# Moving the copy of the last transposed tile behind a weights' cast, and turning two tiles in one go

## The chip, the cores and the metric

The kernel runs on one core of one Trainium2 chip. A core has TensorE (PE: matrix products and transposes through the array), VectorE (DVE), ScalarE (ACT), GpSimd (POOL), SyncE (SP, which here only issues transfers) and 16 DMA engines that move data between the chip's memory and the core's SBUF. The metric is the device time of one launch in microseconds (us), the median of several runs. Each engine takes its instructions strictly in the order in which they stand in the program, so an instruction that waits also holds up what stands behind it.

## The reference

One layer of a hybrid decoder for 512 tokens and a model width of 2048, in float32:

```
h  = rmsnorm(x)
y  = concat[StickBreakingAttn(6 heads), ShortGatedConv(4 groups), GatedDeltaNet(6 heads)](h @ w_in)
x  = x + y @ w_out                                # output projection
x  = x + square(relu(rmsnorm(x) @ w_up)) @ w_down # MLP, width 8192
out = rmsnorm(x)
```

The products keep float32 precision by splitting each operand into a rounded "hi" part (a cast on ACT) and the remainder "lo" (a subtraction on DVE); a product is then three matmuls: hi by hi, hi by lo, lo by hi.

## The kernel before

The program runs through five stages: the input projections with the three mixers (to about 740 us), the output projection (745 to 895 us), the MLP's up products (895 to 1535 us), its down products (to 2147 us) and the final norm. The order of each engine's instructions is fixed when the program is built, by a scheduler that simulates the engines; `behind(...)` tells it that what is issued inside must stand after the given instructions, and `tc.high_priority(...)` lets the preparation of weights move ahead of other work.

**Output projection** (the loop over `m` at L785). For each of 16 blocks of 128 output columns, `gemm` (L129) runs four chunks; a chunk is a load of weights into `raw` (SP), their split into `whi` (ACT, L103) and `wlo` (DVE, L104) and 12 matmuls (L116 to L118). The result is added to x on DVE (L793), giving the tile `x1[m]`. Since the last stage needs x with tokens on partitions, `turn(m)` (L767) transposes the tile by four 128x128 transposes into PSUM (L774) and copies it on ACT into `turned` (L775); after each second tile SP writes `turned` to the scratch tensor `xs` (L777). Before, both tiles of a pair are asked for ahead of the product of block `m`.

**Start of the up products** (`up_pair`, g = 0). The up and down products use a fast scheme with seven products instead of eight, taken in the order 1, 2, 5, 6, 3, 4, 7. Each product is 24 matmuls over eight k-tiles. Products 1 and 2 use weights that were loaded like those of the output projection. The weights of product 5, `W_8784`, are the cast (ACT, L841) and the remainder (DVE, L842) of `q_8786`, a tile that is loaded by SP (L849) and then added to by an accumulating transfer that POOL issues (L865). Product 6 uses `W_8936`, split from the same `q_8786` after DVE has added `q_8782` to it (L859). Between products 2 and 5 PE transposes the last tile, `turn(KT - 1, pbank(2))` (L958). After product 5, `scale_rows` sums squares over partitions by a matmul with ones (L836). Product 4 needs the second half of the normed activations, which goes through memory: `rows` splits it (tile `t22`) and SP writes it to `x22` (L783), and `x4_prep` loads it back in four steps (L900), as `whi` and `wlo`; the last step, `whi_8901` and `wlo_8902`, holds the k-tiles 6 and 7. Its matmuls stand on PE among those of the first product of the next group.

SP carries all these loads and stores in one queue, in a fixed order. A transfer also waits until an earlier one of the same semaphore (one of eight, in turn) has landed.

Of the kernel before, what the change touches and what calls it, by code (L numbers as in the profile page):

```python
# [2 lines left out]

# [13 lines left out]
P = 128  # L17
T = 512
NB = T // P
D = 2048  # L20
KT = D // P
# [6 lines left out]
CHUNK_KT = 4  # L28
# [26 lines left out]
def trunk(ctx, tc, xT, wv1, wv2, wa, wo, wu, wd, vec, wf, out, dbg=None):  # L55
    nc = tc.nc
    V, S, G, PE = nc.vector, nc.scalar, nc.gpsimd, nc.tensor
# [15 lines left out]
    def mmps():  # L73
        pool, bufs = pool_of_mm
        return pool.tile([P, 512], F32, name="mm", tag="mm", bufs=bufs)

    def xps(tag):
        pool, bufs = pool_of[tag]
        return pool.tile([P, 512], F32, name=tag, tag=tag, bufs=bufs)
# [8 lines left out]
    def tmp(n=512):  # L88
        return per.tile([P, n], F32, name="tmp", tag="tmp", bufs=4)

    def big():
        return big_pool.tile([P, 2, 512], F32R, name="big", tag="big", bufs=16, align_bytes=256)
# [4 lines left out]
    def wload(src, n, prio=None):  # L97
        with tc.high_priority(WPRIO if prio is None else prio):
            raw = per.tile([P, 512], F32, name="raw", tag="raw", bufs=4)
            nc.sync.dma_start(out=raw[:, :n], in_=src)  # L100
            hi = per.tile([P, 512], F32R, name="whi", tag="whi", bufs=4, align_bytes=256)
            lo = per.tile([P, 512], F32R, name="wlo", tag="wlo", bufs=4, align_bytes=256)
            S.copy(out=hi[:, :n], in_=raw[:, :n])  # L103
            V.tensor_tensor(out=lo[:, :n], in0=raw[:, :n], in1=hi[:, :n].bitcast(F32), op=ALU.subtract)  # L104
        return hi, lo

    def behind(*ins):

        ctx = ExitStack()
        for i in ins:  # L110
            ctx.enter_context(tc.issue_after(i.ins))
        return ctx

    def mm3(p, lh, ll, rh, rl, first, last, more=False):

        PE.matmul(p, lhsT=lh, rhs=rh, start=first, stop=False, skip_group_check=more)  # L116
        PE.matmul(p, lhsT=lh, rhs=rl, start=False, stop=False, skip_group_check=more)  # L117
        return PE.matmul(p, lhsT=ll, rhs=rh, start=False, stop=last, skip_group_check=more)  # L118

    def gemm_chunk(p, src, acts, c, prio=None):  # L120

        ks = slice(c * CHUNK_KT, (c + 1) * CHUNK_KT)
        hi, lo = wload(src[:, ks, :].rearrange("p k f -> p (k f)"), CHUNK_KT * P, prio)
        for k in range(CHUNK_KT):
            s = slice(k * P, (k + 1) * P)
            a = acts[c * CHUNK_KT + k]
            mm3(p, hi[:, s], lo[:, s], a[:, 0], a[:, 1], c + k == 0, c * CHUNK_KT + k == KT - 1)

    def gemm(src, acts):  # L129
        p = mmps()  # L130
        for c in range(KT // CHUNK_KT):
            gemm_chunk(p, src, acts, c)
        return p

    def silu(x, s):
# [27 lines left out]
    def col(c):  # L163
        return vc[:, c:c + 1]
# [29 lines left out]
    for k in range(KT):  # L194
        hi, lo = wload(wv1[:, k, :], 268, 0)
        xr = big_pool.tile([P, 512], F32, name="xr", tag="xr", bufs=6)
        nc.sync.dma_start(out=xr, in_=xT[:, k, :])
        a = big()
# [4 lines left out]
        for b in range(NB):  # L203
            s = slice(b * P, (b + 1) * P)
# [15 lines left out]
    p = xps("r")  # L220
# [3 lines left out]
    p = xps("r")  # L224
# [90 lines left out]
    p = xps("r")  # L315
# [414 lines left out]
    yh = []  # L730
    for k in ORDER:
        a = big()
# [7 lines left out]
    def half_split(o, src):  # L740
        S.copy(out=o[:, :, 0], in_=src)
        V.tensor_tensor(out=o[:, :, 1], in0=src, in1=o[:, :, 0].bitcast(F32), op=ALU.subtract)
# [8 lines left out]
    def sums(o, A11, A12, A21, A22):  # L751

        sub(o[:, 0], A22, A21)
        nsub(o[:, 1], o[:, 0], A11)
        nsub(o[:, 2], o[:, 1], A12)
        sub(o[:, 3], A11, A21)
# [7 lines left out]
    Rb = per.tile([P, 512], F32, name="Rb")  # L764
    turned = {}

    def turn(m, p=None):  # L767

        if m % 2 == 0:
            turned["o"] = late.tile([P, NB, 2 * P], F32, name="turned", tag="turned", bufs=1)  # L770
        o = turned["o"]
        p = xps("t") if p is None else p
        for b in range(NB):
            PE.transpose(p[:, b * P:(b + 1) * P], x1[m][:, b * P:(b + 1) * P], ident)  # L774
        S.copy(out=o[:, :, m % 2 * P:m % 2 * P + P], in_=p.rearrange("p (b f) -> p b f", b=NB))  # L775
        if m % 2:
            nc.sync.dma_start(out=xs[:, :, (m - 1) * P:(m + 1) * P], in_=o)  # L777

# [6 lines left out]
    for m in range(KT):  # L785
        xr = big_pool.tile([P, 512], F32, name="xr", tag="xr", bufs=6)
        nc.sync.dma_start(out=xr, in_=xT[:, m, :])
        if m == KT - 1 or m and m % 2 == 0:
            for q in range(m - m % 2 - 2 + 2 * (m % 2), m):
                turn(q)  # L790
        p = gemm(wo[m], yh)
        x = big_pool.tile([P, 512], F32, name="x1", tag="xr", bufs=6) if m < KT - 1 else tmp()
        V.tensor_tensor(out=x, in0=p, in1=xr, op=ALU.add)  # L793
        y = tmp()
        S.activation(out=y, in_=x, func=AF.Copy, scale=col(C_N2 + m))
        if m == 0:
            S.activation(out=Rb, in_=x, func=AF.Square)
        else:
            sq = tmp()
            S.activation(out=sq, in_=x, func=AF.Square)  # L800
            if m < KT - 1:
                G.tensor_tensor(out=Rb, in0=Rb, in1=sq, op=ALU.add)
        x1.append(x)
        yw.append(y)
        i = m // 2
        half_split(XP[i][:, m % 2:m % 2 + 1], y[:, :HT].unsqueeze(1))
        if m % 2:
            t = xsum = late.tile([P, 4, HT], F32, name="xsum", tag="xsum", bufs=2)
            y0 = yw[m - 1]
            sums(t, y0[:, :HT], y[:, :HT], y0[:, HT:], y[:, HT:])  # L810
            if m < KT - 1:
                rows(i, t, y)
# [16 lines left out]
    def pbank(n):  # L829
        return psu.tile([P, 512], F32, name="pu", tag={1: "uX", 2: "uY", 4: "uY", 5: "uZ"}[n], bufs=2)  # L830
# [79 lines left out]
    def up_pair(g):  # L910

        st = {}
        z = [per.tile([P, 512], F32, name="raw", tag="raw", bufs=4) for _ in range(2)]
        keep, banks, Ws = {}, {}, {}

        def mms(n, lo, hi):
            p = banks[n]
            for i in range(lo, hi):
                xh, xl = x_side(n, i)
                s = slice(i * P, (i + 1) * P)  # L920
                if isinstance(Ws[n], list):
                    s = slice(i % 4 * P, i % 4 * P + P)
                    w = [a[:, s] for a in Ws[n][i // 4]]
                else:
                    w = [Ws[n][:, 0, s], Ws[n][:, 1, s]]
                last = mm3(p, *w, xh, xl, n in (1, 2, 4, 5) and i == 0, i == KP - 1,
                           n in (6, 7, 3))
            return last

        def take(n):  # L930
            p = banks[n]
            if n in (1, 5, 6, 4):
                keep[n] = tmp()[:, :HT]
                S.copy(out=keep[n], in_=p)
                return
            for o, k in {2: ((z[0][:, :HT], 1),), 3: ((z[1][:, :HT], 6),),
                         7: ((z[0][:, HT:], 4), (z[1][:, HT:], 5))}[n]:
                V.tensor_tensor(out=o, in0=p, in1=keep[k], op=ALU.add)

        src = lambda kh, d: wu[g, kh, d]  # L940
        for n in UP:
            if n not in Ws:
                Ws[n] = w_prep(n, st, src, False, g > 0 or n not in (1, 2))
            if g == 0 and n in (1, 2):
                Ws[n] = [wload(wu[0, n - 1, 0][:, 512 * c:512 * c + 512], 512) for c in range(2)]
            banks[n] = pbank(n)[:, :HT] if n in (1, 2, 4, 5) else banks[{6: 1, 7: 1, 3: 5}[n]]
            if g == 0 and n == 1:
                mms(1, 0, KP - 1)
                continue
            if g == 0 and n == 2:  # L950
                Ws[5] = w_prep(5, st, src, False)
                with behind(*st["split"]):
                    rows(KP - 1, xsum, yw[-1])
                mms(2, 0, KP - 1)
                mms(1, KP - 1, KP)
                take(1)
                with behind(mms(2, KP - 1, KP)):
                    turn(KT - 1, pbank(2))  # L958
                take(2)
                continue  # L960
            else:
                if g == 0 and n == 5:
                    x4_prep()
                last = mms(n, 0, KP)
                if g == 0 and n == 5:
                    scale_rows(last)
            take(n)
        h = ahead.pop("h", None) or h_tile()

        def finish():  # L970
            to_h(g, h, z)

        if g < FF // P // 2 - 1:
            finish()
        else:
            rest.append(finish)
# [273 lines left out]
```

## Time and profile before

| | |
|---|---|
| median of 3 runs | 2159.11 us (2157.95 to 2159.48) |
| the profiled execution, its own time | 2158.76 us |
| its span, from first to last instruction | 2157.1 us |
| PE busy | 2137.5 us, 99% of the span |
| DVE busy | 1661.0 us, 77% |
| ACT busy | 1071.5 us, 50% |
| DMA, share of the hardware queue and of POOL's queue | 41.1% and 13.5% |
| mean granted clock of TensorE | 0.998 |

Columns of a timeline row: start in us, duration in us, engine, line, operation, tile written <- tiles read, shape, count, and in brackets the idle time before it with what ended it. In a table of stretches an engine's number is its busy time in us; PEclk is the clock granted to TensorE (1.00 is 2.4 GHz, 0.50 is 1.2 GHz), the DMA share is that of the 16 engines. Durations overlap where an engine pipelines.

### The profile page before, as it was taken

To read this page: it belongs to the slowest core of one execution; us is meant where nothing else is said; L and a number is where in the kernel's file an instruction comes from. 1 tells how busy PE (TensorE), PEld (TensorE's weight loads), DVE (VectorE), ACT (ScalarE), POOL (GpSimd) and SP (SyncE) were. 2 spreads that over 40 slices of the span, in tenths; PEclk is the share of its full clock that TensorE was granted. 3 is DMA by queue.
4 is the path that set the end of the run, shared out by engine and by line. 5 is a ranking of instruction groups with operands and counts; after the bars stand their busy time and mean duration, and the time that the engine had idled before them with its cause. 6 is when DMAs were issued, how large, how long until landed. Compare 5 with 4: busy or idle time off the path is not lost.

```text
span 2157.1 us, 33102 instructions
## 1 busy us (share of the span) xinstructions
PE 2137.5 (99%) x12674; PEld 1883.5 (87%) x12674; DVE 1661.0 (77%) x2360; ACT 1071.5 (50%) x1629; POOL 132.5 (6%) x188
## 2 busy tenths in 40 slices
PE   9999999999999999999999999999999999999998
PEld 8887888888989888899999999999888888888886
DVE  6677978644656765588788788878998898898897
ACT  5646766333434544444444545444544454444455
POOL 0000000000000011100000000000001000000101
PEclk9999999999999999999999999999999999999999
DMA  5333233222222255766666666666997777787674
GB/s 185 108 99 97 82 92 92 87 93 85 86 79 88 93 162 161 246 189 186 196 188 171 198 196 176 177 199 190 287 306 185 240 223 200 201 228 224 184 214 117
DMA packets 160718, 356.42 MB, mean 165 GB/s; under 512 B 20272, under 2 KB 62256, under 8 KB 160432
## 3 DMA queue, kind: packets, MB, share of 16 engines
q1 hardware_dynamic: 146304, 302.93, 41.1%
q0 software_dynamic: 13968, 50.86, 13.5%
q8 instruction: 99, 1.62, 0.3%
q14 instruction: 59, 0.48, 0.1%
q10 hardware_dynamic: 288, 0.52, 0.1%
HBM read 308.90 MB, written 45.36 MB: 164 GB/s over the span
## 4 chain that ended last, share of the span: by engine, by line
PE 95%; DVE 2%; ACT 1%; DMA 1%; issue 1%; SPq 0%; DVEq 0%; ACTq 0%
PE mm L117 11%; PE mm L116 11%; PE mm L118 11%; PE pu L118 10%; PE pu L116 10%; PE pu L117 10%; PE pp L117 9%; PE pp L118 9%; PE pp L116 9%; PE mm L280 1%; PE mm L281 1%; PE mm L279 1%; PE i L404 1%; DVE W L842 0%; DMA q<-in_wd_dram 0%
## 5 line engine op out<-in xcount | busy, mean ns | idle before, releaser
L841 ACT CAST W<-q 128x1024 fp32r<-128x1024 f32 x446 | 465.0, 1050 | 571.5 <-PE pp L118 261.8
L842 DVE TENSOR_TENSOR W<-q,W 128x1024 fp32r<-128x1024 f32 x446 | 540.7, 1221 | 125.3 <-ACT W L841 121.1
L116 PE MATMUL mm<-big,whi 128*128 128x512 f32 x1024 | 404.6, 395 | 1.8 <-ACT whi L103 1.2
L117 PE MATMUL mm<-big,whi 128*128 128x512 f32 x1024 | 403.9, 394 | 0.0
L118 PE MATMUL mm<-big,wlo 128*128 128x512 f32 x1024 | 402.4, 393 | 0.0
L117 PE MATMUL pp<-W,A 128*128 128x512 f32 x888 | 345.8, 389 | 0.4 <-DVE W L842 0.4
L118 PE MATMUL pp<-W,A 128*128 128x512 f32 x888 | 345.6, 389 | 0.4 <-DVE A L842 0.4
L116 PE MATMUL pp<-W,A 128*128 128x512 f32 x888 | 343.1, 389 | 0.8 <-ACT W L841 0.8
L104 DVE TENSOR_TENSOR wlo<-raw,whi 128x512 fp32r<-128x512 f32 (+1 forms) x292 | 196.8, 675 | 159.4 <-ACT whi L103 151.9
L103 ACT CAST whi<-raw 128x512 fp32r<-128x512 f32 (+1 forms) x292 | 176.8, 607 | 277.0 <-PE mm L117 237.6
L116 PE MATMUL pu<-XS,W 128*128 128x256 f32 x1024 | 287.8, 281 | 1.8 <-ACT W L841 1.6
L118 PE MATMUL pu<-XS,W 128*128 128x256 f32 x1024 | 287.1, 281 | 0.8 <-DVE W L842 0.8
L117 PE MATMUL pu<-XS,W 128*128 128x256 f32 x1024 | 287.2, 280 | 0.0
L116 PEld LDWEIGHTS mm<-big,whi 128*128 128x128 f32 x1024 | 192.4, 188 | 41.4 <-ACT whi L103 1.8
L117 PEld LDWEIGHTS mm<-big,whi 128*128 128x128 f32 x1024 | 192.5, 188 | 39.1 <-DVE big L734 0.3
L118 PEld LDWEIGHTS mm<-big,wlo 128*128 128x128 f32 x1024 | 192.4, 188 | 38.9
L116 PEld LDWEIGHTS pp<-W,A 128*128 128x128 f32 x888 | 166.7, 188 | 36.0 <-ACT W L841 1.5
L117 PEld LDWEIGHTS pp<-W,A 128*128 128x128 f32 x888 | 166.7, 188 | 35.8 <-DVE W L842 1.0
L118 PEld LDWEIGHTS pp<-W,A 128*128 128x128 f32 x888 | 166.7, 188 | 35.2 <-DVE A L842 0.8
L116 PEld LDWEIGHTS pu<-XS,W 128*128 128x128 f32 x1024 | 193.2, 189 | 2.8 <-ACT W L841 2.3
L859 DVE TENSOR_TENSOR q<-q 128x1024 f32<-128x1024 f32 x159 | 193.7, 1219 | 1.3
L118 PEld LDWEIGHTS pu<-XS,W 128*128 128x128 f32 x1024 | 193.1, 189 | 1.0 <-DVE W L842 1.0
(302 smaller groups left out, 3283.5 us busy)
## 6 DMA issues: line engine op xcount, KB each, us to landing
q<-in_wu_dram SPq DMA_DIRECT2D x128, 512.0 KB, 4.5
q<-in_wd_dram SPq DMA_DIRECT2D x128, 512.0 KB, 5.6
raw<-in_wa_dram SPq DMA_DIRECT2D x192, 256.0 KB, 2.9
hs<-h SPq DMA_DIRECT2D x32, 1024.0 KB, 5.5
q<-in_wd_dram POOLq DMA_DIRECT2D x64, 512.0 KB, 7.1
ha<-hs SPq DMA_DIRECT2D x55, 512.0 KB, 6.5
q<-in_wu_dram POOLq DMA_DIRECT2D x33, 512.0 KB, 5.5
raw<-in_wo_dram SPq DMA_DIRECT2D x64, 256.0 KB, 2.9
```

Of the source, the lines that this page charges most:

```text
L103: S.copy(out=hi[:, :n], in_=raw[:, :n])
L104: V.tensor_tensor(out=lo[:, :n], in0=raw[:, :n], in1=hi[:, :n].bitcast(F32), op=ALU.subtract)
L116: PE.matmul(p, lhsT=lh, rhs=rh, start=first, stop=False, skip_group_check=more)
L117: PE.matmul(p, lhsT=lh, rhs=rl, start=False, stop=False, skip_group_check=more)
L118: return PE.matmul(p, lhsT=ll, rhs=rh, start=False, stop=last, skip_group_check=more)
L279: PE.matmul(o, lhsT=xw[k][:, 0, s], rhs=hi[:, ws], start=k == 0 and b % 2 == 0, stop=False)
L280: PE.matmul(o, lhsT=xw[k][:, 0, s], rhs=lo[:, ws], start=False, stop=False)
L281: PE.matmul(o, lhsT=xw[k][:, 1, s], rhs=hi[:, ws], start=False, stop=k == KT - 1 and b % 2 == 1)
L404: PE.matmul(pv[:, b], lhsT=kq[:, 2 * c + b, 0], rhs=kq[:, 2 * c + b], start=True, stop=True)
L841: return (S.copy(out=o[:, 0], in_=src), V.tensor_tensor(out=o[:, 1], in0=src, in1=o[:, 0].bitcast(F32), op=ALU.subtract))
L842: V.tensor_tensor(out=o[:, 1], in0=src, in1=o[:, 0].bitcast(F32), op=ALU.subtract))
L859: on_v = lambda t, u: V.tensor_tensor(out=t, in0=t, in1=u, op=ALU.add)
```

## The change

Two places change. The copy of the last transposed tile is issued behind the split of product 5's weights (`after=st["split"]`), where it stood ahead of it on ACT. And the transposes of a pair of tiles in the output projection are issued together after the second chunk of the following product (`between`), where one tile's stood at the product's start and the other's after its second chunk.

```diff
-            mm3(p, hi[:, s], lo[:, s], a[:, 0], a[:, 1], c + k == 0, c * CHUNK_KT + k == KT - 1)
+            last = mm3(p, hi[:, s], lo[:, s], a[:, 0], a[:, 1], c + k == 0, c * CHUNK_KT + k == KT - 1)
+        return last
...
-    def gemm(src, acts):
+    def gemm(src, acts, between=()):
         p = mmps()
         for c in range(KT // CHUNK_KT):
-            gemm_chunk(p, src, acts, c)
+            last = gemm_chunk(p, src, acts, c)
+            if c == 1 and between:
+                with behind(last):
+                    for f in between:
+                        f()
         return p
...
-    def turn(m, p=None):
+    def turn(m, p=None, after=()):
...
-        S.copy(out=o[:, :, m % 2 * P:m % 2 * P + P], in_=p.rearrange("p (b f) -> p b f", b=NB))
+        with behind(*after):
+            S.copy(out=o[:, :, m % 2 * P:m % 2 * P + P], in_=p.rearrange("p (b f) -> p b f", b=NB))
...
-        if m == KT - 1 or m and m % 2 == 0:
-            for q in range(m - m % 2 - 2 + 2 * (m % 2), m):
-                turn(q)
-        p = gemm(wo[m], yh)
+        turns = range(m - m % 2 - 2 + 2 * (m % 2), m) if m == KT - 1 or m and m % 2 == 0 else ()
+        p = gemm(wo[m], yh, [partial(turn, q) for q in turns])
...
                 with behind(mms(2, KP - 1, KP)):
-                    turn(KT - 1, pbank(2))
+                    turn(KT - 1, pbank(2), st["split"])
```

ACT's order between products 2 and 5, before (`turned_8666` is the copy of the last tile, `W_8784` the cast for product 5, `XS_7227` and `t22_8847` the split of the last activations, `tmp_8875` the copy of product 1's result):

```order
L741 CAST XP_7219<-tmp_8748 128x256
L775 COPY turned_8666<-pu_8880 128x4x128
L841 CAST W_8784<-q_8786 128x1024
L741 CAST XS_7227<-xsum_8754 128x4x256
L741 CAST t22_8847<-tmp_8748 128x256
L934 COPY tmp_8875<-pu_8808 128x256
L841 CAST W_8936<-q_8786 128x1024
```

The same place now (lines of the changed kernel are 6 to 8 higher):

```order
L748 CAST XP_7219<-tmp_8748 128x256
L847 CAST W_8784<-q_8786 128x1024
L748 CAST XS_7227<-xsum_8754 128x4x256
L748 CAST t22_8847<-tmp_8748 128x256
L940 COPY tmp_8875<-pu_8808 128x256
L783 COPY turned_8703<-pu_8880 128x4x128
L847 CAST W_8936<-q_8786 128x1024
```

The copy has moved back by four instructions, and nothing else on ACT has moved here. DVE's order is the same in the whole program.

SP's queue at that time, before (`q_` are weights of the next groups, `xs` is written from the last pair of turned tiles, `x22` from the last `t22`, and `whi_8901` is the first half of product 4's last load):

```order
L849 DMA q_9070<-in_wu_dram 128x1024
L777 DMA xs_7228<-turned_8666 512x1x256
L849 DMA q_9293<-in_wu_dram 128x1024
L783 DMA x22_7229<-t22_8847 128x512
L849 DMA q_9299<-in_wu_dram 128x1024
L849 DMA q_9295<-in_wu_dram 128x1024
L849 DMA q_9522<-in_wu_dram 128x1024
L900 DMA whi_8901<-x22_7229 128x2x256
```

And now:

```order
L855 DMA q_9070<-in_wu_dram 128x1024
L855 DMA q_9293<-in_wu_dram 128x1024
L785 DMA xs_7228<-turned_8703 512x1x256
L791 DMA x22_7229<-t22_8847 128x512
L855 DMA q_9299<-in_wu_dram 128x1024
L855 DMA q_9295<-in_wu_dram 128x1024
L855 DMA q_9522<-in_wu_dram 128x1024
L906 DMA whi_8901<-x22_7229 128x2x256
```

The store to `xs` and one weights' load have changed places; `x22` and `whi_8901` stand where they stood.

PE in the output projection, now, at the first pair whose place has changed (before, the first four transposes stood 24 matmuls earlier, at the product's start):

```order
L118 MATMUL mm_7603<-big_7181,whi_7624 128x512
L119 MATMUL mm_7603<-big_7181,wlo_7625 128x512
L781 MATMUL t_7641<-ident_78,x1_7497 128x128 x4
L781 MATMUL t_7647<-ident_78,x1_7581 128x128 x4
L117 MATMUL mm_7603<-big_7184,whi_7656 128x512
```

Six pairs now stand like this; the number of instructions is the same on every engine.

## Rows read from the trace of the kernel before

**Rows 1.** The page, busy time and share of the span by engine.

```profile
PE 2137.5 (99%) x12674; PEld 1883.5 (87%) x12674; DVE 1661.0 (77%) x2360; ACT 1071.5 (50%) x1629; POOL 132.5 (6%) x188
```

**Rows 2.** All waits of PE from 740 to 915 us: total, times, longest.

```profile
PE pu L116 <- ACT W L841: 1.6, 1, 1.6
PE pu L118 <- DVE W L842: 0.8, 1, 0.8
```

**Rows 3.** Timeline of ACT around the copy of the last tile.

```profile
896.75 0.39 ACT L741 CAST XP<-tmp 128x256 fp32r<-128x256 f32 x1
901.01 0.59 ACT L775 COPY turned<-pu 128x512 f32<-128x512 f32 x1 [3.87 <-PE pu L774]
901.50 1.05 ACT L841 CAST W<-q 128x1024 fp32r<-128x1024 f32 x1
902.44 1.05 ACT L741 CAST XS<-xsum 128x1024 fp32r<-128x1024 f32 x1
...
906.44 1.99 ACT L841 CAST W<-q 128x1024 fp32r<-128x1024 f32 x2 [2.37 <-DVE q L859]
```

**Rows 4.** Timeline of PE: last transposes, starts of products 5 and 6.

```profile
900.38 0.60 PE L774 MATMUL pu<-ident,tmp 128*128 128x128 f32 x4
...
902.60 0.39 PE L116 MATMUL pu<-XS,W 128*128 128x256 f32 x1 [1.62 <-ACT W L841]
...
903.86 0.38 PE L118 MATMUL pu<-XS,W 128*128 128x256 f32 x1 [0.75 <-DVE W L842]
...
909.22 0.29 PE L118 MATMUL pu<-XS,W 128*128 128x256 f32 x1
```

**Rows 5.** Timeline of DVE: the weights of products 5 and 6.

```profile
902.58 1.23 DVE L842 TENSOR_TENSOR W<-q,W 128x1024 fp32r<-128x1024 f32 x1 [3.56 <-ACT W L841]
...
905.19 1.22 DVE L859 TENSOR_TENSOR q<-q 128x1024 f32<-128x1024 f32 x1
...
907.52 2.36 DVE L842 TENSOR_TENSOR W<-q,W 128x1024 fp32r<-128x1024 f32 x2 [0.78 <-ACT W L841]
```

**Rows 6.** Stretches: us, engines' busy time, then granted clock, DMA share, GB/s.

```profile
66.00:70.00 4.00, 3.00 (x14) 1.84 (x14) 1.39 (x2) 2.89 (x6) 1.04 (x1) 1.00 0.34 114
900.00:904.00 4.00, 1.63 (x12) 1.18 (x11) 1.43 (x2) 2.99 (x5) 0.00 (x0) 1.00 1.04 396
905.00:909.00 4.00, 4.00 (x18) 3.29 (x17) 3.22 (x5) 2.26 (x3) 0.00 (x0) 0.57 1.07 404
909.00:916.00 7.00, 7.00 (x61) 7.00 (x60) 4.93 (x6) 4.52 (x6) 0.00 (x0) 1.00 1.04 407
```

**Rows 7.** Timeline of POOL: accumulating transfers for the first and the second group.

```profile
890.92 1.01 POOL L865 DMA_DIRECT2D q<-in_wu_dram  x1 [4.06 <-DMA q<-in_wu_dram]
...
918.74 0.88 POOL L871 DMA_DIRECT2D q<-in_wu_dram  x1 [20.34 <-DVE q L859]
```

**Rows 8.** Line L865, issue to landing of its only transfer.

```profile
DMA to landing us min/median/max: 7.8/7.8/7.8
```

**Rows 9.** Timeline of SP: the last store to x22 and its load back.

```profile
907.98 0.36 SPq L783 DMA_DIRECT2D x<-t  x1
...
915.82 0.38 SPq L900 DMA_DIRECT2D whi<-x  x1
```

**Rows 10.** Line L900 at 915.8 us, issue to landing of that load.

```profile
DMA to landing us min/median/max: 4.3/4.3/4.3
```

**Rows 11.** Timeline of PE: the first matmul on that load.

```profile
920.23 0.35 PE L116 MATMUL pu<-whi,W 128*128 128x256 f32 x1
```

**Rows 12.** The page, POOL's queue: packets, MB, share of 16 engines' span.

```profile
q0 software_dynamic: 13968, 50.86, 13.5%
```

**Rows 13.** Timeline of PE, output projection: the left-out rows include four transposes.

```profile
762.52 0.39 PE L116 MATMUL mm<-big,whi 128*128 128x512 f32 x1
...
762.97 0.39 PE L118 MATMUL mm<-big,wlo 128*128 128x512 f32 x1
...
764.10 0.40 PE L118 MATMUL mm<-big,wlo 128*128 128x512 f32 x1
```

More of the change, by code (lines that the diff above doesn't have):

```diff
@@ L2 @@
 from contextlib import ExitStack
+from functools import partial
 import numpy as np
```

## The prediction

> **What bounds the kernel now.** First the page's table of engines: PE is busy 99% of the span [rows 1], so a change is worth what it does to PE's idle time or to PE's pace, and only if PE does not stop later for something else. Then PE's waits in the output projection and at the start of the up products: over 175 us there are two, 1.6 and 0.8 us, both at the first matmuls of product 5, and none in the loop where the pairs of tiles are turned [rows 2]. Then the timelines around them. ACT is free from about 897.1 us (896.75 + 0.39) but stands in front of the copy of the last tile, which waits 3.87 us for PE's last transposes; the cast for product 5 stands behind and starts at 901.50 [rows 3]. PE ends the transposes at 900.98, gets the hi part at 902.60 and the lo part, after DVE's 1.23 us, at 903.86 [rows 4, 5]. Last the table of stretches: in 900 to 904 us PE works 1.63 of 4 us, and in 905 to 909 us it is busy all the time at a granted clock of 0.57 on average, that is mostly at 1.2 GHz; from 909 on it is back at 1.00 [rows 6]. That fall costs 4 x (1 - 0.57) = 1.7 us on top of the stall. In 900 to 916 us the DMA engines are full (shares of 1.04 to 1.07 at about 400 GB/s) [rows 6]. Keep that in mind: what PE needs from memory there comes at the DMA's pace, not at PE's.
>
> **The copy behind the cast.** Nothing is added or removed; one copy of 0.59 us goes four places back on ACT, and SP's store of the pair goes one place back. What decides when the cast can start is then its input: the accumulating transfer, issued at 890.92 and landed 7.8 us later, at 898.7 [rows 7, 8]. So the cast starts at about 898.75, 2.75 us earlier, and ends at 899.8. DVE's lo part, free of other work since before it began to wait (its 3.56 us idle start at 899.0), runs 899.85 to 901.05 [rows 5]. PE ends its transposes at 900.98 and does hi by hi and hi by lo first, so it starts product 5 without a wait: 1.62 + 0.75 us of idle go, its first lo matmul goes from 903.86 to 901.2.
>
> What is late next is product 6. Its weights come through a chain on DVE and ACT that has no room: lo of product 5, two splits, the addition into the same tile (905.19), the cast (906.44), the lo part (907.52, its half of two done at 908.74) [rows 3, 5]. Each follows the other at once, so the chain moves by the same 2.75 us and its end goes to 906.0. PE would be there at about 904.8 (product 5 at full clock, 24 matmuls in 2.8 us, and the sum over partitions, about 1 us), so it now waits about 1 us for DVE. Its first lo matmul of product 6 goes from 909.22 [rows 4] to about 906.05. Gain up to here 3.2 us: more than the idle of 2.4, since the 1.7 us of slow clock go as well, less the new wait of 1. A pause of this size did not lower the clock elsewhere: in 66 to 70 us PE is idle for 1.0 of 4 us at 1.00 [rows 6].
>
> From there PE runs without a wait to its first matmul on the last piece of `x22`, at 920.23 [rows 11]. It would now arrive at 917.05. But that piece is issued at 915.82 and lands 4.3 us later, at 920.1: in the kernel before it came 0.1 us ahead of its use [rows 9 to 11]. Does it come earlier now? Its place in SP's queue is the same; ahead of it stand the same bytes, with a store and a load exchanged. The last store to `x22` is ready earlier (its split on DVE by 2.75 us), but it is issued at 907.98 in a queue that is behind: full DMA engines from 900 on, each transfer waiting for an older one to land. The three weights' loads between the store and the load back are still there. So I take 920.1 for the landing, and the gain of 3.2 us shrinks to 920.23 - 920.15 = 0.1 us; the idle time is now one piece of 3.1 us, from 917.05 to 920.15.
>
> And the clock: a pause of 2.4 us within 2.9 us was followed by 1.7 us lost. A pause of 3.1 us in one piece should be followed by the same, so I put 1.7 us back on, after 920. Bounds: 0 (it stays up, as after 1.0 us idle) and 1.7 or somewhat more; I take 1.6, nearest to the only row of a pause as long.
>
> Behind the cast nothing else gets a new wait that matters: the copy of the last tile now runs at about 901.3, and its PSUM bank is wanted by the sum over partitions at 903.8; the store to `xs` is read only in the last stage.
>
> **The pairs in one go.** Four transposes stand between two matmuls whose starts are 764.10 - 762.97 = 1.13 us apart with two further matmuls; at 0.225 us a matmul the four cost 0.455 us [rows 13]. Eight in one go cost at most twice that, and save at most the overlap lost at one change between transposes and matmuls, a few hundredths. Six pairs: 0 to -0.2 us, I take -0.1. They now need x1 of the block before, which DVE has added 5 us earlier, and the copies stand on ACT at half load while the casts run chunks ahead; PE has no wait there now [rows 2], and I expect none.
>
> **The sum.** 2158.8 us (the profiled execution) - 0.1 (product 4's load decides) + 1.6 (clock) - 0.1 (pairs) = 2160.2, I write 2160.3. The profiled execution lies 0.3 us below the median of the three runs, within their spread of 1.5.
>
> **Rivals.**
> - *The clock stays up.* All as above, but 3.1 us of waiting leave the clock at 1.00: 2158.8 - 0.1 - 0.1 = 2158.6. For it speaks that the fall came after two pauses with transposes ahead of them, of which there is one example; against it that this pause is longer.
> - *The load comes early and the gain stays.* If the store to `x22` or the load back lands 3 us sooner (say because the exchanged store of 1 KB pieces now stands behind a load), PE does not stop at 917: 2158.8 - 3.2 - 0.1 = 2155.5. For it: the split is ready sooner. Against: 16 us of full DMA engines, and five transfers fixed in order.
> - *The next accumulating transfer gets in the way (slower).* POOL issues it at 918.74, when DVE has done an addition that follows PE [rows 7]. With PE 3.2 us ahead it goes out at 915.5, before the load back has even been issued. Such a transfer costs 0.135 x 2157.1 us over 50.86 MB / 0.524 MB = 97 transfers, that is 3.0 us of all 16 engines [rows 12]. If its packets go first, the piece of `x22` lands at up to 923.1, and with the clock's fall the sum is 2158.8 - 0.1 + 3.0 + 1.6 - 0.1 = 2163.2. It decides once PE is more than about 1.5 us early at the start of group two. Before, it was issued 1.4 us ahead of the landing and did not show. The Trainium skill (DMA: Bandwidth & Descriptors, "Queues, rings and completion order") says that a DMA engine takes turns between the queues it has work for, packet by packet; by that rule about half of the 3.0 us would fall before the landing and the time would be 2161.7. No row here shows the packets, so I keep 0 and 3.0 as the ends, and 0 to 0.5 as the likely part.
> - *The change does not take hold.* The cast waits for something the row hides (its queue entry is only seen after 901): 2158.8 - 0.1 = 2158.7.
>
> **How the numbers follow.** Forecast 0.45, with a range of its own of 2159.4 to 2161.5; clock stays up 0.2; load comes early 0.14; accumulating transfer 0.17; does not take hold 0.04. About 0.2% (4.3 us) is what a measurement of this kernel can tell from no change, and hardly any case reaches it: faster than 2154.8 needs the whole gain and more (0.04), slower than 2163.4 needs the whole transfer in front, the clock's fall and an unlucky run (0.07). The range runs from the early load, 2155.5, to the transfer in front, 2163.2.
>
> **What the profile after would show.** Right: ACT's cast for product 5 ahead of the copy, starting at 898.7 to 899; no wait of PE before product 5 and clock 1.00 in 905 to 909; a wait of about 1 us on DVE at product 6; a wait of about 3 us at the first matmul on the last load (now L117, on a DMA), near 917 to 920; a clock of about 0.5 for some 3 us after it; POOL's accumulating transfer at about 915.5; the loop of the output projection without waits. Wrong: no wait at that matmul (the gain stays), a landing at 922 or later (the transfer in front), or any wait of PE between 760 and 895 us (the pairs cost something).

## The result and the profile after

| | before | after |
|---|---|---|
| median, runs of one comparison | 2158.99 us (2157.39 to 2160.64, 14 runs) | 2162.84 us (2159.43 to 2165.14, 14 runs) |
| ratio, 95% interval | | 1.0015 [1.0008, 1.0022] |
| the profiled execution | 2158.76 us | 2162.31 us |

The change makes the kernel 3.9 us slower by the medians (1.7 to 4.8 by the interval). One run of the experiments below, of the kernel with the pause filled, took 3560.65 us at a mean granted clock of 0.555, and the ratios are those of the other runs. PE's busy time is that of before less 1.2 us [rows 1]; the time went into waiting.

The page of the changed kernel, engines:

```profile
PE 2136.3 (99%) x12674; PEld 1882.2 (87%) x12674; DVE 1660.7 (77%) x2360; ACT 1071.6 (50%) x1629; POOL 132.8 (6%) x188
```

PE's waits from 740 to 960 us. The two of [rows 2] are gone, and one wait on a transfer, the last piece of `x22`, is longer than both together:

```profile
PE pu L117 <- DMA whi<-x: 5.8, 1, 5.8
PE pu L119 <- DVE W L848: 0.3, 1, 0.3
```

ACT, to be held against [rows 3]. The cast for product 5 now waits for its input alone and starts 4.24 us earlier; the copy comes behind it:

```profile
897.26 1.05 ACT L847 CAST W<-q 128x1024 fp32r<-128x1024 f32 x1 [0.55 <-DMA q<-in_wu_dram]
...
900.90 0.59 ACT L783 COPY turned<-pu 128x512 f32<-128x512 f32 x1
...
902.44 2.00 ACT L847 CAST W<-q 128x1024 fp32r<-128x1024 f32 x2 [0.94 <-DVE q L865]
```

DVE [rows 5]. The chain to the weights of product 6 has moved by 4.0 us (907.52 to 903.52):

```profile
898.51 1.21 DVE L848 TENSOR_TENSOR W<-q,W 128x1024 fp32r<-128x1024 f32 x1
...
903.52 2.36 DVE L848 TENSOR_TENSOR W<-q,W 128x1024 fp32r<-128x1024 f32 x2 [0.78 <-ACT W L847]
```

PE [rows 4, 11]. Product 5 follows the transposes at once, product 6 gets its lo part at 904.80 instead of 909.22, and the last matmul ahead of the wait ends at 916.09; then nothing until 921.89, where the kernel before was at 920.23:

```profile
899.94 0.60 PE L781 MATMUL pu<-ident,tmp 128*128 128x128 f32 x4
900.30 0.36 PE L117 MATMUL pu<-XS,W 128*128 128x256 f32 x1
...
904.80 0.39 PE L119 MATMUL pu<-XS,W 128*128 128x256 f32 x1 [0.31 <-DVE W L848]
...
915.81 0.28 PE L118 MATMUL pu<-XP,W 128*128 128x256 f32 x1
921.89 0.58 PE L117 MATMUL pu<-whi,W 128*128 128x256 f32 x1 [5.81 <-DMA whi<-x]
```

The stretches (columns as in [rows 6]: busy time of PE, weight loads, DVE, ACT and POOL, then the clock, the DMA share and GB/s):

```profile
900.00:904.00 4.00, 4.00 (x32) 3.61 (x30) 3.22 (x5) 2.42 (x4) 0.00 (x0) 1.00 1.04 396
905.00:909.00 4.00, 4.00 (x35) 4.00 (x35) 2.83 (x3) 2.19 (x4) 0.00 (x0) 1.00 1.07 407
909.00:916.00 7.00, 7.00 (x60) 6.89 (x59) 4.43 (x5) 2.41 (x4) 0.88 (x1) 1.00 1.03 402
916.00:920.00 4.00, 0.09 (x1) 0.00 (x0) 1.23 (x1) 0.59 (x1) 0.00 (x0) 1.00 1.02 218
920.00:922.00 2.00, 0.10 (x1) 0.11 (x1) 0.00 (x0) 0.00 (x0) 0.00 (x0) 0.84 1.07 392
922.00:925.00 3.00, 3.00 (x15) 3.00 (x16) 0.00 (x0) 0.14 (x1) 0.00 (x0) 0.54 0.11 42
```

Read them in two halves. Up to 916 all is better than before: PE busy 4.00 of 4 us at the start where it was 1.63, and the clock 1.00 in 905 to 909 where it was 0.57. From 916 on PE stands, while the DMA engines are full (1.02) and yet move only 218 GB/s, half of what they moved up to 916. When PE starts again, at 921.89, the clock is at its lower level until about 924.6. The kernel before has neither the pause nor the slow clock there, and its DMA engines come down to that rate (0.99 at 204 GB/s) only from 920 on, when the first half of the piece has landed:

```profile
916.00:920.00 4.00, 4.00 (x36) 4.00 (x35) 2.41 (x2) 0.15 (x1) 0.88 (x1) 1.00 0.93 309
920.00:922.00 2.00, 2.00 (x19) 2.00 (x18) 1.07 (x1) 0.96 (x2) 0.00 (x0) 1.00 0.99 204
922.00:925.00 3.00, 3.00 (x28) 3.00 (x27) 2.14 (x5) 1.62 (x3) 0.00 (x0) 1.00 0.63 116
```

What filled the engines shows on POOL and SP [rows 7, 9]. The second group's accumulating transfer goes out at 914.44 instead of 918.74, now 0.55 us ahead of the load of the piece instead of 2.9 us behind it. SP issues that load when the last store to `x22` has landed, 8.3 us after its own issue at 906.66 (before, 7.8 us after 907.98):

```profile
890.27 1.01 POOL L871 DMA_DIRECT2D q<-in_wu_dram  x1 [3.83 <-DMA q<-in_wu_dram]
...
914.44 0.88 POOL L877 DMA_DIRECT2D q<-in_wu_dram  x1 [16.48 <-DVE q L865]
```

```profile
906.66 0.55 SPq L791 DMA_DIRECT2D x<-t  x1
...
914.99 0.38 SPq L906 DMA_DIRECT2D whi<-x  x1
```

and the two halves of that load, L906, take 6.9 and 7.1 us to land where the first took 4.3 [rows 10]:

```profile
DMA to landing us min/median/max: 6.9/7.0/7.1
```

The balance by marks on PE: first matmul on the last piece 920.23 to 921.89, +1.66 us; from there to the first matmul on `XS` of the second group 5.84 us before (to 926.07), 7.19 after (to 929.08), +1.35 more, the slow clock in this execution; first matmul of the down products 1534.17 to 1537.26, +3.1; whole executions +3.55. Of the 3.55 us, 3.01 have happened by 929 us; 0.46 come behind the start of the down products and were not traced.

### The profile page after: what moved, and what is told of

It is laid out like the page before. It is cut to its first block, busy times and chain, and to the rows that moved or that the text cites. A ratio compares the mean times of both kernels' runs of the same rounds, so it can differ in the third digit from the quotient of the medians.

```text
span 2160.6 us, 33101 instructions
## 1 busy us (share of the span) xinstructions
PE 2136.3 (99%) x12674; PEld 1882.2 (87%) x12674; DVE 1660.7 (77%) x2360; ACT 1071.6 (50%) x1629; POOL 132.8 (6%) x188
## 4 chain that ended last, share of the span: by engine, by line
PE 93%; DMA 2%; DVE 2%; ACT 1%; issue 1%; SPq 0%; DVEq 0%; ACTq 0%
PE mm L118 11%; PE mm L117 11%; PE mm L119 11%; PE pu L117 9%; PE pu L119 9%; PE pu L118 9%; PE pp L118 9%; PE pp L119 9%; PE pp L117 9%; PE mm L287 1%; PE mm L288 1%; PE mm L286 1%; DMA ha<-hs 1%; PE i L411 1%; DVE W L848 0%
## 5 line engine op out<-in xcount | busy, mean ns | idle before, releaser
L865 DVE TENSOR_TENSOR q<-q 128x1024 f32<-128x1024 f32 x159 | 193.8, 1220 | 1.9 <-DMA q<-in_wd_dram 0.5
```

Source lines behind the costliest of these rows:

```text
L865: on_v = lambda t, u: V.tensor_tensor(out=t, in0=t, in1=u, op=ALU.add)
```

## The experiments

All were timed beside the kernel before. One theory and three rivals stood at the outset. *Collision*, the theory: the transfer that POOL issues when PE comes early takes the DMA engines from the load that PE needs next. Rivals: the pairs of transposes cost the time; the pause and the clock alone cost it; or the order of SP's queue does.

**One part alone: the copy.** The kernel before with only the copy behind the split:

```diff
-                    turn(KT - 1, pbank(2))
+                    turn(KT - 1, pbank(2), st["split"])
```

> Only the copy of the last tile moves behind the cast; the pairs are turned as before. If the slowdown comes from the load of product 4's last piece meeting POOL's accumulating transfer, and from the clock's fall behind the wait, all of it is here: 3.5 to 4.5 us over the kernel before, PE waiting 5 to 6 us for that load, POOL's transfer issued about 4 us earlier than in the kernel before, and a stretch at about 0.5 of the clock after the wait. If the pairs are to blame, the time is that of the kernel before or up to 3.7 us below it.

2163.81 us (11 runs), ratio 1.0017 [1.0008, 1.0026]: as much as the whole change lost. PE waits 6.92 us for the piece, and POOL's transfer is early here too:

```profile
914.93 0.88 POOL L872 DMA_DIRECT2D q<-in_wu_dram  x1 [16.47 <-DVE q L860]
```

```profile
923.50 0.58 PE L116 MATMUL pu<-whi,W 128*128 128x256 f32 x1 [6.92 <-DMA whi<-x]
```

**The other part alone: the pairs.** The changed kernel with the copy where it was:

```diff
-                    turn(KT - 1, pbank(2), st["split"])
+                    turn(KT - 1, pbank(2))
```

> Only the pairs are turned in one go; the copy stands before the cast, as in the kernel before. By the first theory the time is 0 to 0.4 us below the kernel before, with the old stall of 2.4 us before product 5 and POOL's transfer at about 918.5 us. If the pairs are to blame: 3 to 4 us above it.

2158.84 us (11 runs), ratio 0.9994 [0.9985, 1.0003]. No difference that can be measured; the old waits are back and POOL's transfer is late again:

```profile
PE pu L117 <- ACT W L847: 1.6, 1, 1.6
PE pu L119 <- DVE W L848: 0.8, 1, 0.8
```

```profile
918.55 0.88 POOL L877 DMA_DIRECT2D q<-in_wu_dram  x1 [20.39 <-DVE q L865]
```

**The transfer held back, with a confound.** POOL copies one column of the last piece into a new tile first; its transfer stands behind that copy, so it cannot go out before the piece has landed.

```diff
+    seen = per.tile([P, 1], F32, name="seen")
...
+        held.append(G.tensor_copy(out=seen, in_=X4[-1][1][:, 511:512].bitcast(F32)))
...
+                    with behind(held.pop()):
                         nc.gpsimd.dma_start(out=st["x"], in_=src(1, 1), accum_op=ALU.add)
```

> The changed kernel, but POOL reads one column of product 4's last piece before it issues the second group's accumulating transfer, so that this transfer cannot start before the piece has landed. If the two collide, the piece lands at 919 to 920 instead of 921.9, PE waits 3 to 4 us instead of 5.8, the clock still falls, and the time is 1.5 to 2.5 us below the changed kernel, still 1 to 2.5 us above the kernel before. If the exchanged store and load in SP's queue delay the piece, nothing changes: 3.9 us above the kernel before.

2141.81 us (4 runs), ratio 0.9914 [0.9901, 0.9928]: 18 us faster than before, far beyond the theory and its rivals. Locally it did as the theory said: the transfer goes out at 920.02, the load lands in 4.3 us, PE waits 3.49 us.

```profile
919.52 0.19 POOL L914 COPY seen<-wlo 128x1 f32<-128x1 f32 x1 [21.96 <-DMA wlo<-x]
920.02 0.88 POOL L879 DMA_DIRECT2D q<-in_wu_dram  x1 [0.31 <-issue]
```

The 18 us lie elsewhere: in matmuls of the up products hundreds of us later, each 4 ns shorter. By line, operation and shape over the whole program (count, busy us, mean ns) this kernel has

```profile
L117 PE MATMUL pu<-XS,W 128*128 128x256 f32 x1024 | 283.8, 277 | 0.2 <-ACT tmp L947 0.2
L117 PE MATMUL pu<-XP,W 128*128 128x256 f32 x496 | 137.5, 277 | 0.0
```

and the changed kernel

```profile
L117 PE MATMUL pu<-XS,W 128*128 128x256 f32 x1024 | 287.3, 281 | 0.2 <-ACT tmp L940 0.2
L117 PE MATMUL pu<-XP,W 128*128 128x256 f32 x496 | 139.0, 280 | 0.0
```

From start to start of neighbouring matmuls it is 113.5 ns against 117.4. The new tile's 4 bytes take 32 in SBUF, and with them the tiles `XP` and `XS` start 32 bytes higher. 4560 such matmuls x 3.9 ns = 17.8 us. So this run says nothing about the transfer's price, and two more had to separate the two causes.

**The transfer held back, nothing moved in SBUF.** The same, the column written into a tile that exists and is no longer read:

```diff
-        held.append(G.tensor_copy(out=seen, in_=X4[-1][1][:, 511:512].bitcast(F32)))
+        held.append(G.tensor_copy(out=lns_c, in_=X4[-1][1][:, 511:512].bitcast(F32)))
```

> The changed kernel, with the second group's first accumulating transfer held on POOL behind a one-column copy that reads the last transposed tile, as in e3, but the column is written into a tile that exists already, so that no operand moves in SBUF. Theory (the accumulating transfer's 512 KB stand in the DMA engines while the X4 tiles are loaded, and TensorE pays for it): the wait for the first whi tile falls from 5.8 us to about 3.5 us as in e3, its load lands in about 4.3 us, pu matmuls keep the pitch of 117 ns, and the time is 1.5 to 2.5 us below the changed kernel: 2160.3 to 2161.3, 1.3 to 2.3 us above the kernel before. Rival 1 (e3's 18 us came from the order of the transfers): about 2142 again. Rival 2 (the collision costs nothing in the end, since the pause of TensorE and the clock's fall come anyway): about 2162.8.

2160.27 us (11 runs), ratio 1.0005 [0.9996, 1.0014]: 0.7 us above the kernel before, about 2 to 3 below the changed one, though the two intervals overlap at their ends. The load lands in 4.3 us again, with the store and the load in SP's queue exchanged as in the changed kernel, so the rival of SP's order falls:

```profile
920.33 0.58 PE L117 MATMUL pu<-whi,W 128*128 128x256 f32 x1 [3.77 <-DMA whi<-x]
```

This is the forecast's case, made: the load at its old pace, a pause of 3.8 us, the clock at 0.50 behind it (until 926), and a time near the kernel before. Two of the stretches:

```profile
922.00:923.00 1.00, 1.00 (x6) 1.00 (x6) 0.00 (x0) 0.00 (x0) 0.45 (x1) 0.50 0.00 0
924.00:925.00 1.00, 1.00 (x7) 1.00 (x7) 0.63 (x1) 0.61 (x2) 0.00 (x0) 0.50 1.01 172
```

But the profiled execution, 2162.26 us, is one of the slowest of the 11. From the first matmul on the piece to `XS` of the second group it takes 8.45 us (920.33 to 928.78) where the changed kernel took 7.19, because the clock stays at 0.50 for longer; what the load gained is lost again in this execution. The copy alone took 8.57 us there (923.50 to 932.07). So one execution's slow clock costs 1.35 us and another's 2.6 to 2.7, and the transfer's price in the whole time rests on the medians; what the profiles show is the landing, 4.3 us against 6.9.

**The place in SBUF alone.** The changed kernel with the extra tile and no other edit:

```diff
+    pad = per.tile([P, 1], F32, name="pad")
+    G.memset(pad, 0.0)
```

> The changed kernel with one more 4-byte tile, which moves the start of the XP and XS tiles up by 32 bytes in SBUF; the order of the instructions is that of the changed kernel but for one memset at the start of the program. Theory (e3's gain of 18 us beyond its transfer is the place of the moving operand in SBUF, 117.4 to 113.5 ns of pitch on some 4480 matmuls): about 2145 (17 to 18 us below the changed kernel), the X4 wait still 5.8 us. Rival (the gain belonged to the later transfer or to the copy that reads the tile): 2162.8, as the changed kernel.

2145.81 us (5 runs), ratio 0.9940 [0.9927, 0.9952], 17 us below the changed kernel by the medians. The wait is still there (4.5 us for the first half of the piece, 0.7 for the second), so the two causes are separate. The rows by shape:

```profile
L117 PE MATMUL pu<-XS,W 128*128 128x256 f32 x1024 | 283.5, 277 | 0.2 <-ACT tmp L942 0.2
L117 PE MATMUL pu<-XP,W 128*128 128x256 f32 x496 | 137.8, 278 | 0.0
```

**The pause filled.** 46 unused matmuls stand where PE waited, and the remaining matmuls on the last piece come behind them.

```diff
+                    for f in range(46):
+                        with behind(last):
+                            last = PE.matmul(pp_x[:, 0, :HT], lhsT=XP[0][:, 0, 0, :P], rhs=XP[0][:, 0, 0, :], start=True, stop=True)
```

> The changed kernel with 46 extra matmuls (128x256, 5.4 us, results unused) on PE between product 7 and the matmuls on product 4's last piece, that is in the time in which PE would wait for it. If the pause makes the clock fall, the clock stays at 1.00 behind it and the time is 1 to 2 us below the changed kernel in spite of the extra work. If the clock falls for another reason, the time is that of the changed kernel or up to 1 us more.

2161.94 us (11 runs), ratio 1.0012 [1.0003, 1.0021]. With PE busy until 920.84 the clock stays at 1.00 over the rest of the wait and behind it, but the whole time does not tell this kernel from the changed one, and the 1 to 2 us less that were expected do not show:

```profile
915.17 5.67 PE L977 MATMUL pp<-XP 128*128 128x256 f32 x46
...
921.88 0.39 PE L117 MATMUL pu<-whi,W 128*128 128x256 f32 x1 [1.04 <-DMA whi<-x]
```

The stretches of PE alone (busy time, clock, DMA share, GB/s):

```profile
921.00:922.00 1.00, 0.12 (x1) 1.00 0.82 321
922.00:925.00 3.00, 2.69 (x21) 1.00 0.05 16
```

Its next group starts on `XS` at 928.90 against 929.08: the edit puts five matmuls (0.6 us) that stood ahead of the wait behind it, and adds two short waits. So it shows that the idle time is what lowers the clock; the price of that is read from the marks above, not from this run.

**The wait taken away.** The last piece is split straight into SBUF, where it is needed, instead of going through `x22`; the next groups' loads stand behind the remaining loads from `x22`, and the copies of the first results behind the cast.

```diff
+        if i == KP - 1:
+            hl = [per.tile([P, 512], F32R, name=n, tag=n, bufs=4, align_bytes=256) for n in ("whi", "wlo")]
+            S.copy(out=hl[0][:, HT:], in_=y[:, HT:])
+            V.tensor_tensor(out=hl[1][:, HT:], in0=y[:, HT:], in1=hl[0][:, HT:].bitcast(F32), op=ALU.subtract)
...
+                    with behind(*(x4_loads if st.get("g") in (2, 3) or st.get("g") == 1 and k >= NQ else ())):
                         st[q] = quarter(src(*quarters[q]), q)
```

> The changed kernel, with the last of the X4 operands split straight into SBUF instead of stored to x22 and read back, and the loads of the next groups' weights held behind the X4 loads. Theory (what the copy's move gains is lost at the X4 wait alone): without that wait the gain of about 3.5 us up to product 6 stays, and the clock does not fall there: 2154 to 2156.5, 2.5 to 5 us below the kernel before. Rival (the time is lost again further on, at the loads of the next groups' weights): 2159 or more.

2155.00 us (11 runs), ratio 0.9979 [0.9970, 0.9988]: 4.5 us faster than before. One wait of 0.7 us is left in 740 to 960 us; POOL's transfer is as early as in the changed kernel (914.79), PE does not stop, and the clock stays up:

```profile
916.00:920.00 4.00, 4.00 (x36) 4.00 (x36) 3.66 (x7) 2.67 (x4) 0.00 (x0) 1.00 1.04 315
920.00:922.00 2.00, 2.00 (x19) 2.00 (x18) 1.91 (x4) 0.34 (x1) 0.00 (x0) 1.00 0.35 74
```

The 4.5 us are the size of the 4.4 that PE gains up to product 6 (909.22 to 904.80). So the copy's move brings what it gains up to 916, if nothing behind it stops PE, as far as this run can tell: it has three edits more, and the kernel before with these three alone was not run.

**Both together.** That kernel with the 32 bytes of padding:

> e9 with the 32 bytes of e10. If both theories hold they add: 2136 to 2139. If the place in SBUF is not the cause, as e9.

2138.13 us (4 runs), ratio 0.9902 [0.9889, 0.9916]: 21 us below the kernel before, the best version here. The two gains add.

**Further places.** Two kernels on top of that one ask what about the place matters. In the first `XP` and `XS` start at 0 and 64 in steps of 256 bytes (they were at 192; in the kernels before and after at 160):

```diff
+    pad0 = late.tile([P, 16], F32, name="pad0")
     XP = [late.tile([P, 2, 2, HT], F32R, name="XP", tag="XP", bufs=KP) for i in range(KP)]
+    pad1 = late.tile([P, 16], F32, name="pad1")
     XS = [late.tile([P, 4, 2, HT], F32R, name="XS", tag="XS", bufs=KP) for i in range(KP)]
```

> e11 with XP moved on to a start of 0 and XS to a start of 64 in steps of 256 bytes (both were at 192, and at 160 in the kernels before and after). Theory (what matters is that the moving operand starts on a multiple of 64 bytes): the pitch of both stays at 113 to 114 ns and the time at 2136 to 2141. Rival (it matters that the moving tile's place differs from the stationary W's, which starts at 0): the pitch of XP rises to 120 ns, that of whi, which starts at 0 too; with one third of some 4480 matmuls, 1500 x 6.4 ns is 9.6 us: about 2148.

2159.23 us (10 runs), ratio 1.0003 [0.9993, 1.0012]. All of the gain from the place is gone: 119.7 ns for `XP` and 117.9 for `XS`. The theory of multiples of 64 falls. The rival holds for `XP` alone: at 64 `XS` starts elsewhere than W and is slow too, and the time is 11 us above the rival's 2148. In the second the W tiles start at 192 instead of 0:

```diff
-        return mlp.tile([P, 2, 1024], F32R, name="W", tag="W", bufs=3, align_bytes=256)
+        return mlp.tile([P, 2, 1024], F32R, name="W", tag="W", bufs=3, align_bytes=64)
...
+            padw = mlp.tile([P, 48], F32, name="padw")
```

> e11 with the W tiles moved from 0 to 192 in steps of 256 bytes. W is the stationary operand of the up products and the moving one of the down products. Theory (multiples of 64 bytes are all alike): no change, 2136 to 2141, pitch of the down products 227 ns for 512 columns. Rival (places alike in both operands cost, or 0 is a bad start): the down products' 2630 matmuls lose or gain up to 6 ns each, 16 us either way, and the up products change too.

2180.49 us (4 runs), ratio 1.0102 [1.0087, 1.0117]: 42 us more than with W at 0. `XP` and `XS` are at 120 ns (from 113.5), `whi` at 117.5 (from 120), and a down product's 512 columns at 233.4 ns (from 226.7). From these, 4560 x 6.4 - 768 x 2.5 + 2664 x 6.7 ns = 45 us.

## Why the prediction came near, and by another way

The time, 2162.84, is inside the range, at its upper end; the forecast, 2160.3, is not what happened. What happened is the third rival, the accumulating transfer, which was given 0.17; the time lies in the range because this rival's price set the range's upper end.

- *The cast starts when its input lands; both waits and the slow clock of 905 to 909 go.* Right. The landing was put at 898.7 and came at about 897.2: the transfer was issued 0.65 us earlier (890.92 to 890.27) and landed in 7.0 us, not 7.8.
- *A new wait of 1 us at product 6, gain there 3.2 us.* The wait is there, 0.31 us; the gain is 4.4 (909.22 to 904.80), since the chain of weights moved by 4.0 us, not by 2.75.
- *The load of the last piece lands at 920.1 as before, and the gain shrinks to 0.1 us.* **This is the step that failed.** It was right that this load decides and that nothing of the gain survives it. But its landing was taken from the kernel before, with 0 to 0.5 us as the likely part of the accumulating transfer. The prediction had seen that this transfer's issue hangs on DVE and so on PE, and that it would go out ahead of the load; it priced it by the kernel before, where the transfer, issued 2.9 us behind the load, did not show. The load was issued 0.8 us earlier than before and took 2.6 us longer; the term was not -0.1 but +1.66. Over the runs the order of the two issues goes with the landing:

| kernel | POOL's transfer issued | load issued | first half lands after |
|---|---|---|---|
| before | 918.74 | 915.82 | 4.3 us |
| pairs alone | 918.55 | 915.34 | 4.3 us |
| held back, nothing moved | 921.57 | 915.98 | 4.3 us |
| held back, with the confound | 920.02 | 914.49 | 4.3 us |
| changed | 914.44 | 914.99 | 6.9 us |
| copy alone | 914.93 | 916.55 | 6.9 us |
| pause filled | 914.23 | 914.96 | 6.9 us |
| 32 bytes | 913.95 | 914.11 | 5.8 us (the second half 7.9) |

  Of the 3.0 us of engine time that the prediction worked out for such a transfer, 2.6 show as the load's delay. By the Trainium skill's rule (DMA: Bandwidth & Descriptors, "Queues, rings and completion order"), turns between queues packet by packet, about half was expected. The trace of the changed kernel agrees in kind, since both queues move data all the while: from 916 to 920 the engines took 131 packets of POOL's queue and 234 of SP's. But they spent 74% of their time on POOL's and 28% on SP's: equal turns need not be equal time, and the estimate of half took them so. Which engine took which packet, and whether the packets counted here are those of the rule, these rows do not show. The rows for 916 to 920 (queue, packets, MB, share of 16 engines' time):

```profile
q0 software_dynamic: 131, 0.49, 74.3%
q1 hardware_dynamic: 234, 0.38, 27.8%
```

- *The clock falls again, 1.6 us.* Right: 1.35 us in the profiled execution, at 0.54 on average from 922 to 925, and 2.6 to 2.7 in two other kernels' executions. In all five runs with a pause of 3.5 to 6.9 us at that load it fell; with the pause filled, or without one, it stayed at 1.00 there. The rival in which it stays up falls.
- *The pairs: -0.1 us.* Right in size, within what can be measured, but it does not belong in the sum: what PE gains ahead of the load is lost at the load, by the prediction's own third step. The projection ends 0.44 us earlier (894.88 to 894.44), of which 0.18 was there before the first pair.

With the two sizes put right the sum is 2158.8 + 1.66 + 1.35 = 2161.8; the profiled execution took 2162.3. The 0.5 us between them were not traced. The load was issued at times between 914.1 and 916.6 in different kernels, which moves the result by as much as the clock does. In each the load waits for the landing of the last store to `x22`: 907.98 + 7.8 us before, 906.66 + 8.3 in the changed kernel, 907.28 + 9.2 with the copy alone. Why that store takes longer in one kernel than in another was not settled. SP's wait for it, in the kernel before and in the changed one (905 to 918 us):

```profile
SPq L900 <- DMA x<-t: 2.0, 1, 2.0
SPq L906 <- DMA x<-t: 5.1, 1, 5.1
```

That the early load would keep the gain, the second rival, was made true only by taking the load away (4.5 us faster).

## What to carry to other kernels

Before a stall is removed, list what the stalled engine's progress releases elsewhere: a transfer whose issue follows it will move by the same time, and may then collide with a load that was just in time. A landing read from the trace holds only for the order of issues in that trace. And when an experiment gives far more than any theory allows, look for what else it moved: here an added tile of 4 bytes.

## What was not expected of the hardware

**The pace of a float32r matmul depends on where its operands start in SBUF.** Starts are those of the compiled kernels, in bytes modulo 256; the times are means from start to start, in neighbouring matmuls of one operand:

| moving operand at | stationary at | columns | ns from start to start |
|---|---|---|---|
| `XP`, `XS` 192 | W 0 | 256 | 113.5 |
| `XP`, `XS` 160 | W 0 | 256 | 117.4 |
| `XS` 64 | W 0 | 256 | 117.9 |
| `whi` 0 | W 192 | 256 | 117.5 |
| `XP` 0 | W 0 | 256 | 119.7 |
| `whi` 0 | W 0 | 256 | 120 |
| `XP`, `XS` 192 | W 192 | 256 | 120 |
| W 0 | A 0 | 512 | 226.7 |
| W 192 | A 0 | 512 | 233.4 |

For 256 columns the pace goes with the difference of the two starts (0: 120; 64: 117.5 to 118; 160: 117.4; 192: 113.5). With 512 columns the same difference of 192 is the slower one, so the difference alone is not the rule; what it is stays open. The best against the worst is 6%, and on an engine that is busy 99% of the time that is more than the change under study by an order of magnitude.

**An accumulating transfer fills the DMA engines at less than half their rate.** In the kernel with the transfer held back it runs alone: a share of 1.01 at 172 GB/s from 924 to 925, where plain loads show 1.03 to 1.07 at 402 to 407 up to 916. Its 0.52 MB took 51.1% of the engines' time from 922 to 928, that is 3.1 us of all 16, as the prediction had worked out (3.0).

```profile
q0 software_dynamic: 144, 0.52, 51.1%
```
